# First attention: exponentials copied to the rounded type between queues, transposed one unit later, and one scratch space for all scores

## The chip, the cores and the metric

The kernel runs on one core of a Trainium2 chip. The metric is the device time of one execution in microseconds (us), the median of the runs shown. PE is the matrix engine (PEld its weight loads), ACT, DVE and POOL are the three engines for elementwise work, SP is the engine that issues most of the transfers (DMAs). Each engine has a list of instructions of its own, whose order is fixed when the program is built.

## The reference

One encoder layer for two sequences of 2048 tokens with 1024 features. What matters here:

```python
h = rms_norm(x, norm_w); proj = h @ w_in          # q_a k_a v_a g_a q_b k_b v_b g_b
o_a = windowed_gqa_sink(q_a, k_a, v_a, sink_a) * jax.nn.silu(g_a)   # "first attention"
o_b = neighbourhood_attn(q_b, k_b, v_b, rpb_b) * jax.nn.silu(g_b)   # "second attention"
x = x + jnp.concatenate([o_a, o_b], axis=-1) @ w_out
return x + (p @ w_ple) * jax.nn.sigmoid(x @ w_ple_gate)

# windowed_gqa_sink, for a block of 128 queries, 8 query heads, 2 key heads:
sc = jnp.einsum('bqkgd,bskd->bkgqs', qb, kb) * scale   # keys within +-128 tokens
sc = jnp.where(valid, sc, -jnp.inf)
m = jnp.maximum(jnp.max(sc, axis=-1, keepdims=True), sink_f)
e = jnp.exp(sc - m)
denom = jnp.sum(e, axis=-1, keepdims=True) + jnp.exp(sink_f - m)
o = jnp.einsum('bkgqs,bskd->bqkgd', e / denom, vb)
```

Everything is 32-bit. The kernel keeps that precision by splitting each operand of a product into a rounded high part (the type `float32r`, "the rounded type") and a low part, and adding the products of the parts.

## The kernel before

**Three stretches.** The first attention fills the first 750 us or so, the second attention runs to about 1800 us, and the output products fill the rest. This case is about the first.

**Tiles and units.** The first attention takes the 4096 tokens in 32 tiles of 128 (index `f`; `t` is the tile within its sequence of 16). Each tile has two units, one for each key head (`kv` 0 and 1). A tile whose neighbours on both sides exist (`left and right`) has the full window; four tiles of the 32 lie at an end of a sequence. In a unit (`unit_a`):

- `sc(i)`, i = 0 to 3: two products give the scores of 128 rows by 320 keys into PSUM; DVE (`softmax`, L295) adds the mask, writes the scores to SBUF and takes the row maximum. Two calls make a pair of 640 columns. After the fourth, `exps` runs: DVE makes `nm`, the negated maximum (L316), and ACT makes four exponentials in place (L319).
- `pt(j)`, j = 0 to 2: PE transposes the exponentials in blocks of 128x128 into PSUM (`tr`, L282): two blocks for j = 0, four for j = 1 and four for j = 2, ten in all. ACT copies them out as the high part of `pr` (L757) and DVE subtracts to make the low part (L759). For j = 0 both go in two halves of 64 partitions.
- `po(j)`: the products of `pr` with the values `vv`, high part then low part: four products of 256 columns for j = 0 and for j = 1, two of 512 columns for j = 2.
- `den`: the reciprocal of the denominator and the gate (`g2`). `fin`: PE transposes `g2` (`pgt`), ACT and DVE fold the halves of `po` and multiply, SP stores the result (`oa_d`).
- `prep` (once per tile): PE transposes the next tile's queries (`pqt`), `rest` finishes their split.

**The filler.** Between these steps PE works on the projections of a later tile, as a stream of products: `pk` (24 of 256 columns), `pq` and `pg` (24 of 512 columns each). Their operands come from `xr`, a split tile of x, loaded by SP (`stx`, and `stn` for the sums of squares).

**What sets the order.** A table `PLAN_A` gives for each step its place within the unit, as a share of the stream's cost, and whether it belongs to this unit (`now` = 1) or to the unit before it (0). So a step is put into PE's order behind so many products of the stream. The order of the other engines follows from a scheduler at build time that keeps data dependencies and the priorities of the program. What it made of ACT's and DVE's lists is shown below with the change.

**The types of a transpose.** `tr` transposes data of the type that it finds. In the first attention the exponentials are plain 32-bit floats; in most units of the second attention (`copied_`) ACT issues a DMA that copies each exponential into a tile `tn` of the rounded type (L328), and PE transposes that (L280).

**Buffers.** The scores of the first attention lie in `s2` (three slots of 640 columns). A tag `s` of five buffers of 512 columns serves early loads, the scores of the second attention and results of the last stretch. PSUM has three buffers for `sc`, `pt` and `pgt`, and two for `po`, `pqt` and the keys (`pkt`).

Of the kernel before, what the change touches and what calls it, by code (L numbers as in the profile page):

```python
# [58 lines left out]
def bias_offsets():  # L59
# [31 lines left out]
CP = 2  # L91
KB = 23
PLAN_A = (
    (0.04, 1, "sc", 0), (0.10, 1, "sc", 1), (0.12, 1, "sc", 2), (0.12, 1, "rest", 0), (0.14, 1, "sc", 3),
    (0.14, 1, "rest", 1), (0.14, 0, "po", 0),
    (0.22, 0, "po", 1), (0.34, 0, "po", 2), (0.45, 0, "fin", 0), (0.46, 1, "prep", 0), (0.58, 1, "den", 0),
    (0.75, 1, "pt", 0), (0.79, 1, "pt", 1), (0.88, 1, "pt", 2),
)
PLAN_B = (
# [13 lines left out]
    return 2 * NT <= f and not (4 * NT - 9 <= f < 4 * NT - 5 or f >= 6 * NT - 9)  # L113


def plan(f):

    def of(k):
        return PLAN_A if k < 2 * NT else PLAN_C if copied_(k) else PLAN_B
    if f <= 2 * NT:  # L120
        return of(f)
    return sorted([x for x in of(f - 1) if not x[1]] + [x for x in of(f) if x[1]], key=lambda x: x[0])


def emit(ctx, tc, io):
# [12 lines left out]
    rowwise = cp.tile([128, 128], F32R, tag="rowwise", name="rowwise")  # L138
    nc.gpsimd.tensor_copy(rowwise.rearrange("p (r c) -> p r c", c=16), ident.rearrange("p (c r) -> p r c", r=8))
# [8 lines left out]
    wkt = cp.tile([128, 4], F32, tag="wkt", name="wkt")  # L148
    nc.scalar.dma_start(wkt, io["qk_norms"])

    main = ctx.enter_context(tc.tile_pool(name="main", bufs=1))
# [139 lines left out]
    def softmax(i, ps, n, bias, sm, s=None):  # L291

        if s is None:
            s = main.tile([128, 512], F32, tag="s", name="s", bufs=SB)[:, :n]
        nc.vector.tensor_tensor_reduce(out=s, in0=ps[:, :n], in1=bias, scale=1.0, scalar=-3.0e38,  # L295
                                       op0=ALU.add, op1=ALU.max, accum_out=sm["mx"][:, i:i + 1])
        sm["s"].append(s)
# [70 lines left out]
        loads += [("n", f, 0), ("n", f, 1)] if f < 2 * NT else []  # L368
    loads, staged = iter(loads), {}

    def load_block(key, tag, bufs):
        kind, f, i = key
        staged[key] = main.tile([128, 512], F32, tag=tag, name="st" + kind, bufs=bufs)
# [61 lines left out]
    for i in range(2):  # L435
        raws_x += load_first(st[1][:, 2 * i:2 * i + 2], 4 + 2 * i, 0, 256)
    for i in range(2):
        load_block(("x", 1, i), "s", SB)
    raws_q += load_first(main.tile([128, 2, 512], F32, tag="p_t", name="ws", bufs=3), 0, 256, 512)
    raw = ap.tile([128, 4, 512], F32, tag="raw", name="ws", bufs=1)  # L440
    raws_q += load_first(raw[:, 0:2], 2, 256, 512)
    raws_q += load_first(raw[:, 2:4], 4, 256, 512)
    raws_q += load_first(main.tile([128, 2, 512], F32, tag="p_t", name="ws", bufs=3), 6, 256, 512)
    for i in range(2):
        load_block(("n", 0, i), "s", SB)
    for j in range(4):
        raws_g += load_first(ap.tile([128, 1, 512], F32, tag="qg", name="wg", bufs=6), j, 768, 512)
    cs = main.tile([128, 2, NT, 16], F32, tag="s", name="cs", bufs=SB)
    nc.sync.dma_start(cs, io["rope"])
    rw = ap.tile([128, 4, 16], F32, tag="rw", name="rw")  # L450
    nc.sync.dma_start(rw, io["rope_w"].partition_broadcast(128))
# [251 lines left out]
        qrest[f] = split_q(pqt, q1, q2, 1)  # L703
        return q1, q2

    p_rot, s2, tn = [], [], []

    def unit_a(f, kv):
        s, t = divmod(f, NT)
# [63 lines left out]
        def fin(_):  # L773
# [9 lines left out]
            for e in range(2):  # L783
# [2 lines left out]
            nc.vector.tensor_tensor(out=ot, in0=pgt, in1=ot, op=ALU.mult)  # L786
            nc.sync.dma_start(oa_d[s].rearrange("(i p) q -> p i q", p=128)[:, 2 * kv:2 * kv + 2, 128 * t:128 * t + 128],
                              ot)
        return {"sc": sc, "pt": pt, "po": po, "fin": fin, "prep": lambda _: nxt(f) if kv else None,
                "den": lambda _: next(got["ex"]), "rest": lambda _: None if kv else next(qrest[f])}  # L790

    pending = []
# [271 lines left out]
    def ple_ahead(n, tail=False):  # L1064

        load_p(n + 1)
        for m in range(KT):
            if m % 4 == 3 and (n < 3 or m == 3):
                load_coming()
            ps = ptile([128, TW], "pj", "pple")  # L1070
            if m == 5 and n + 1 < len(tiles):
                split_p(n + 1)
            flush("p0")
            for k in range(2):
                w, c = early["p"][2 * (m // 4) + k], 128 * (m % 4)
                for i, (a, b) in enumerate(((0, 0), (0, 1), (1, 0))):
                    mm(ps, w[:, a, c:c + 128], p_rs[n][:, k, b], k == 0 and i == 0, k == 1 and i == 2)
                    yield 215
            if tail:
                ev = main.tile([128, TW], F32, tag="s", name="ev", bufs=SB)  # L1080
            else:
                if not evs:
                    evs.extend([ap.tile([128, 3, 640], F32, tag="ev", name="ev", bufs=1), 0])
                if m // 2 % 2:
                    ev = ap.tile([128, TW], F32, tag="sq", name="ev", bufs=2)
                else:
                    ev = evs[0][:, evs[1] % 3, :TW]
                    evs[1] += 1
            P(nc.scalar.copy(ev, ps))
            store_ple(1)  # L1090
            if tail:
                nc.sync.dma_start(ple_d[n][:, m], ev)
            else:
                made.append((ple_d[n][:, m], ev))
# [72 lines left out]
    for f in range(6 * NT):  # L1167
# [7 lines left out]
        spent = 0  # L1175
        for kv in range(2 if in_a else 1):
            unit = unit_a(f, kv) if in_a else unit_b(f)
            for part, now, act, i in plan(f):
# [6 lines left out]
        while spent < total:  # L1185
            spent += next(stream, total)
        if f in (2 * NT - 1, 6 * NT - 1):
            for part, now, act, i in PLAN_A if in_a else PLAN_B:
# [14 lines left out]
    with tc.tile_pool(name="c", bufs=1, reuse_waits="tile") as op:  # L1203
# [132 lines left out]
        def result(n, i, mi, ps):  # L1336
# [3 lines left out]
            first, final = i not in (1, 4, 5), i not in (0, 2, 3)  # L1340
            V = nc.vector
            if first:
                r = main.tile([128, TW], F32, tag="s", name="r", bufs=SB) if count[1] % 9 < SB else \
# [164 lines left out]
```

## Time and profile before

| | us |
|---|---|
| median of three runs (2453.13 to 2453.51) | 2453.3 |
| profiled execution | 2451.72 |
| its span, first to last instruction | 2449.9 |
| busy: PE / PEld | 2437.0 / 2061.1 |
| busy: DVE / ACT / POOL | 1706.2 / 1413.3 / 851.0 |

The span is what the profile shows instruction by instruction; the profiled execution's own time is 1.8 us more, and the median of the runs 1.6 us more than that. PE counts as busy for 99% of the span, but its instructions overlap in the record: a transpose is recorded with 272 ns, and four in a row start about 109 ns apart. What an instruction costs PE is the distance from its start to the next start, not its recorded duration.

### The profile page before, as it was taken

What the parts mean: (1) busy time and instruction counts of PE and PEld (TensorE: products, weight loads), DVE (VectorE), ACT (ScalarE), POOL (GpSimd) and SP (SyncE); (2) the same over time, 40 slices, a digit from 0 to 9 for tenths busy, and PEclk for the clock granted to TensorE, in tenths of its full rate; (3) what the DMA queues carried; (4) which work ended last, traced back from release to release, by engine and by line L of the source; (5) the groups of instructions that cost most, each with busy time, mean ns of one, the idle gap of its engine ahead of it and who ended that gap; (6) DMA issues with size and microseconds to landing.
All of it is one profiled execution on the core that took longest, in us unless ns stands there. A gap on an engine that the chain in (4) does not pass through costs nothing.

```text
span 2449.9 us, 40820 instructions
## 1 busy us (share of the span) xinstructions
PE 2437.0 (99%) x13062; PEld 2061.1 (84%) x13062; DVE 1706.2 (70%) x4214; ACT 1413.3 (58%) x3408; POOL 851.0 (35%) x1363
## 2 busy tenths in 40 slices
PE   9999999999999999999999999999999999999999
PEld 8888888888888888888888888888888888888887
DVE  7777777777775666666666677776537655677776
ACT  7777767776755555666656666666753222344443
POOL 4555555555543544555444444443100000000000
PEclk9999999999999999999999999999999999999999
DMA  6323223232353677768966687787887445855765
GB/s 229 123 97 100 92 92 103 94 95 89 104 181 125 209 240 246 235 213 261 309 213 227 224 271 261 247 266 248 302 273 259 162 157 183 268 184 203 249 224 171
DMA packets 275254, 479.64 MB, mean 196 GB/s; under 512 B 31168, under 2 KB 116064, under 8 KB 270816
## 3 DMA queue, kind: packets, MB, share of 16 engines
q1 hardware_dynamic: 245376, 437.84, 53.8%
q10 hardware_dynamic: 29664, 39.19, 5.2%
q8 instruction: 104, 1.70, 0.3%
q14 instruction: 110, 0.90, 0.1%
HBM read 307.72 MB, written 134.23 MB: 180 GB/s over the span
## 4 chain that ended last, share of the span: by engine, by line
PE 91%; DVE 3%; DMA 3%; ACT 2%; POOL 1%; issue 1%; SPq 0%; DVEq 0%; ACTq 0%; POOLq 0%
PE pvg L276 15%; PE pqk L276 14%; PE acca L1311 14%; PE accc L1311 10%; PE pq L276 6%; PE pg L276 6%; PE scb L276 3%; PE pob L276 3%; PE po L276 3%; PE pple L276 3%; PE pk L276 3%; PE sc L276 3%; PE pt L282 2%; PE ptb L280 2%; DMA vw<-v_d 1%; DVE pr L759 1%
## 5 line engine op out<-in xcount | busy, mean ns | idle before, releaser
L276 PE MATMUL pvg<-wb,xr 128*128 128x512 f32 x1536 | 470.4, 408 | 0.3 <-DMA wb<-sp_1wb 0.3
L276 PE MATMUL pqk<-wa,xr 128*128 128x512 f32 x1536 | 431.1, 408 | 0.0
L319 ACT ACTIVATE s<-s,nm 128x320 f32<-128x320 f32 (+6 forms) x512 | 293.2, 574 | 148.5 <-DVE nm L316 118.0
L276 PEld LDWEIGHTS pvg<-wb,xr 128*128 128x128 f32 x1536 | 273.0, 189 | 33.2 <-DMA wb<-sp_1wb 0.8
L276 PEld LDWEIGHTS pqk<-wa,xr 128*128 128x128 f32 x1536 | 265.0, 188 | 39.2
L1293 ACT CAST opd<-raw 128x512 fp32r<-128x512 f32 x224 | 131.5, 619 | 270.7 <-PE acca L1311 117.8
L397 POOL TENSOR_TENSOR xr<-stx,xr 128x512 fp32r<-128x512 f32 x186 | 238.0, 1296 | 103.5 <-ACT xr L396 72.9
L1294 DVE TENSOR_TENSOR opd<-raw,opd 128x512 fp32r<-128x512 f32 x224 | 146.4, 685 | 146.2 <-ACT opd L1293 146.2
L276 PE MATMUL pg<-wb,xr 128*128 128x512 f32 x768 | 233.4, 410 | 1.3 <-DVE vv L554 1.0
L276 PE MATMUL pq<-wa,xr 128*128 128x512 f32 x768 | 219.3, 400 | 0.0
L295 DVE CUSTOM_DVE_ANT_0 s<-scb,bias 128x288 f32<-128x288 f32 (+3 forms) x256 | 138.8, 547 | 71.8 <-PE scb L276 51.6
L993 ACT COPY otb<-pob 64x512 f32<-64x512 f32 x128 | 74.3, 581 | 182.7 <-PE pob L276 182.0
L1311 PE MATMUL accc<-opd,wb 128*128 128x512 f32 x768 | 176.7, 389 | 0.0
L1311 PE MATMUL acca<-opd,wa 128*128 128x512 f32 (+1 forms) x780 | 175.9, 386 | 0.5 <-ACT r L1389 0.5
L1311 PE MATMUL acca<-opd,s 128*128 128x512 f32 x768 | 175.4, 389 | 0.0
L1311 PEld LDWEIGHTS acca<-opd,wa 128*128 128x128 f32 x780 | 145.0, 188 | 30.2 <-ACT r L1389 0.7
L1311 PEld LDWEIGHTS acca<-opd,s 128*128 128x128 f32 x768 | 144.1, 188 | 29.9
L1311 PEld LDWEIGHTS accc<-opd,wb 128*128 128x128 f32 x768 | 144.1, 188 | 29.9
L161 POOL TENSOR_TENSOR yb<-vrb,power 128x8 f32<-128x8 f32 x64 | 106.4, 1662 | 150.6 <-DVE vrb L831 137.7
L276 PEld LDWEIGHTS pq<-wa,xr 128*128 128x128 f32 x768 | 135.1, 189 | 17.3
L759 DVE TENSOR_TENSOR pr<-pt,pr 128x512 fp32r<-128x512 f32 (+2 forms) x248 | 135.3, 549 | 16.5 <-ACT pr L757 13.1
L276 PEld LDWEIGHTS pg<-wb,xr 128*128 128x128 f32 x768 | 131.9, 189 | 17.4 <-DVE vv L554 1.4
(177 smaller groups left out, 5141.4 us busy)
## 6 DMA issues: line engine op xcount, KB each, us to landing
stx<-x_b SPq DMA_DIRECT2D x128, 256.0 KB
vw<-v_d SPq DMA_DIRECT2D x96, 256.0 KB
stx<-x_a SPq DMA_DIRECT2D x64, 256.0 KB
stn<-x_n SPq DMA_DIRECT2D x64, 256.0 KB
v_d<-vb SPq DMA_DIRECT2D x64, 256.0 KB
ple_d<-ev SPq DMA_DIRECT2D x64, 256.0 KB
xres<-x_r SPq DMA_DIRECT2D x64, 256.0 KB
x_d<-r SPq DMA_DIRECT2D x64, 256.0 KB
```

The lines of the kernel that those rows point to most:

```text
L161: nc.gpsimd.tensor_tensor(out=y, in0=v, in1=power.broadcast_to([128, n]), op=ALU.pow)
L276: pinned(nc.tensor.matmul(out, lhsT, rhs, start=start, stop=stop))
L280: pinned(nc.tensor.transpose(out.bitcast(F32R), in_, eye))
L282: pinned(nc.tensor.transpose(out, in_, eye.bitcast(F32)))
L295: nc.vector.tensor_tensor_reduce(out=s, in0=ps[:, :n], in1=bias, scale=1.0, scalar=-3.0e38, op0=ALU.add, op1=ALU.max, accum_out=sm["mx"][: ...
L319: ex = nc.scalar.activation(ss[i], ss[i], AF.Exp, bias=nm[:, i:i + 1], accum_out=den[:, i:i + 1])
L397: low.tensor_tensor(out=lo, in0=raw, in1=hi.bitcast(F32), op=ALU.subtract)
L759: nc.vector.tensor_tensor(out=pr[r, 1, to], in0=pt[r, c], in1=pr[r, 0, to].bitcast(F32), op=ALU.subtract)
L993: nc.scalar.copy(ot[a:a + 64], pq[z:z + 64])
L1293: P(nc.scalar.copy(hi, v))
L1294: P(nc.vector.tensor_tensor(out=lo, in0=v, in1=hi.bitcast(F32), op=ALU.subtract))
L1311: pinned(nc.tensor.matmul(ps[:, cols], w[k][:, a, c:c + 128], o[:, b, cols], start=i in (0, 1, 4) and k == 0 and j == 0, stop=k == 3 and j ...
```

## The change

In tiles with both neighbours, the exponentials of a pair (128x640) are copied by a DMA that SP issues (`turn`) into a tile `tna` of the rounded type, three slots of 640 columns, and the transposes read that. The copies are ordered at 0.39 of the unit; `pt` moves from 0.75 to 0.88 of the same unit to 0.24, 0.31 and 0.38 of the next one; `po` moves from 0.14, 0.22 and 0.34 of the next unit to 0.52, 0.60 and 0.72; `fin` from 0.45 to 0.80, `prep` from 0.46 to 0.66 and `den` from 0.58 to 0.74. The places of `sc` become 0.04, 0.08, 0.11, 0.14. The four end tiles make no copy and are transposed as before in type, at the new places. The last unit keeps `pt` within itself (`PLAN_L`).

`tna` takes the room of `s2`. The scores of the first attention now lie in four slots of 640 columns of one tile `space`, which also replaces the five buffers of the tag `s` everywhere (`s_tile`). The identity matrix is built in that space and kept in the rounded type.

```diff
 PLAN_A = (
-    (0.04, 1, "sc", 0), (0.10, 1, "sc", 1), (0.12, 1, "sc", 2), (0.12, 1, "rest", 0), (0.14, 1, "sc", 3),
-    (0.14, 1, "rest", 1), (0.14, 0, "po", 0),
-    (0.22, 0, "po", 1), (0.34, 0, "po", 2), (0.45, 0, "fin", 0), (0.46, 1, "prep", 0), (0.58, 1, "den", 0),
+    (0.04, 1, "sc", 0), (0.08, 1, "sc", 1), (0.11, 1, "sc", 2), (0.12, 1, "rest", 0), (0.14, 1, "sc", 3),
+    (0.14, 1, "rest", 1), (0.24, 0, "pt", 0), (0.31, 0, "pt", 1), (0.38, 0, "pt", 2), (0.39, 1, "turn", 0), (0.39, 1, "turn", 1),
+    (0.52, 0, "po", 0), (0.60, 0, "po", 1), (0.66, 1, "prep", 0), (0.72, 0, "po", 2), (0.74, 1, "den", 0), (0.80, 0, "fin", 0),
+)
+PLAN_L = tuple((part, now or act == "pt", act, i) for part, now, act, i in PLAN_A if act != "pt") + (
     (0.75, 1, "pt", 0), (0.79, 1, "pt", 1), (0.88, 1, "pt", 2),
 )
...
-    ident = cp.tile([128, 128], F32, tag="ident", name="ident")
-    make_identity(nc, ident)
...
+    space = main.tile([128, SB * 512], F32, tag="s", name="s")
+    taken = [0]
+
+    def s_tile():
+
+        k = taken[0] % SB
+        taken[0] += 1
+        return space[:, 512 * k:512 * k + 512]
+
+    eye32 = space[:, 512 * SB - 128:512 * SB]
+    make_identity(nc, eye32)
+    ident, rowwise = (cp.tile([128, 128], F32R, tag=n, name=n) for n in ("ident", "rowwise"))
+    nc.vector.tensor_copy(ident, eye32)
...
+        def turn(pair):
+
+            if left and right:
+                if len(s2) < 3:
+                    s2.append(ap.tile([128, 3, 640], F32R, tag="ev", name="tna", bufs=1))
+                to = s2[2][:, s2[1] % 3]
+                s2[1] += 1
+                nc.sync.dma_start(to.bitcast(F32), pairs[pair])
+                pairs[pair] = to
+
         def sc(i):
...
             if half == 0:
-                if not s2:
-                    s2.extend([ap.tile([128, 3, 640], F32, tag="ev", name="s2", bufs=1), 0])
-                pairs.append(s2[0][:, s2[1] % 3])
-                s2[1] += 1
+                k = 640 * (s2[0] % 4)
+                pairs.append(space[:, k:k + 640])
+                s2[0] += 1
```

How the rows of three engines move. PE, in the unit of key head 0 of an inner tile, from the last scores to the first value products (`pq` is the filler); before:

```order
L276 MATMUL sc<-ks_a,q_292 128x320
L276 MATMUL po<-pr,vv 128x256 x4
L276 MATMUL pq<-wa_106,xr 128x512
L276 MATMUL pq<-wa_107,xr 128x512
L276 MATMUL po<-pr,vv 128x256 x4
L276 MATMUL pq<-wa_107,xr 128x512 x2
L276 MATMUL pq<-wa_108,xr 128x512 x2
L276 MATMUL po<-pr,vv 128x512 x2
```

and with the change:

```order
L288 MATMUL sc<-ks_a,q_289 128x320
L288 MATMUL pq<-wa_108,xr 128x512
L288 MATMUL pq<-wa_109,xr 128x512 x2
L292 MATMUL pt<-ident,tna 128x128 x2
L288 MATMUL pq<-wa_109,xr 128x512
L288 MATMUL pq<-wa_110,xr 128x512
L292 MATMUL pt<-ident,tna 128x128 x4
L288 MATMUL pq<-wa_110,xr 128x512 x2
L292 MATMUL pt<-ident,tna 128x128 x4
L288 MATMUL pq<-wa_111,xr 128x512 x3
L288 MATMUL pq<-wa_112,xr 128x512
L288 MATMUL po<-pr,vv 128x256 x4
```

The value products used to follow the last scores at once, with transposes made in the unit before; now the transposes of the unit before stand between them, with eleven filler products from the last scores to the first `po`, and three from `po(0)` to `po(1)`. In the unit of key head 1 the list is alike with `pg` as filler: also eleven up to `po(0)`, then two of `pg` and one of `pk` up to `po(1)`.

ACT, the same unit (`s` are the exponentials, `pr` the copies out of the transposes); before:

```order
L354 CAST q_2991<-pqt 64x512
L319 ACTIVATE s_656,den<-s_656,nm 128x320 x4
L334 ACTIVATE es<-es 128x4
L782 COPY ot<-po 64x2x2x64 x2
L553 ACTIVATE vv<-pk,y 128x2x64
L757 CAST pr<-pt 64x256 x2
L599 ACTIVATE sq<-pq 128x512
L757 CAST pr<-pt 128x512 x2
```

and with the change, first in the unit of key head 0 and then in that of key head 1:

```order
L366 CAST q_4880<-pqt 64x512
L331 ACTIVATE s,den<-s,nm 128x320 x4
L346 ACTIVATE es<-es 128x4
L778 CAST pr<-pt 64x256 x2
L778 CAST pr<-pt 128x512 x2
L565 ACTIVATE vv<-pk,y 128x2x64
L803 COPY ot<-po 64x2x2x64 x2
```

```order
L534 ACTIVATE ks_a<-pkt,wk 64x128 x2
L778 CAST pr<-pt 64x256 x2
L331 ACTIVATE s,den<-s,nm 128x320 x4
L346 ACTIVATE es<-es 128x4
L778 CAST pr<-pt 128x512 x2
```

Behind the exponentials of a unit ACT used to copy `po` out; now it copies the transposes of the unit before: in the unit of key head 0 all four copies stand behind the four exponentials, in that of key head 1 the two copies of `pt(1)` and `pt(2)` do.

DVE, the unit of key head 0 with the change, from `nm` on (`gs` is a gate, 128x512):

```order
L328 SCALAR_TENSOR_TENSOR nm<-mx,snk 128x4
L345 TENSOR_TENSOR es<-snk,nm 128x4
L368 TENSOR_TENSOR q_289<-pqt,q_3015 64x512
L581 TENSOR_SCALAR vr<-ssq,ee 128x2
L780 TENSOR_TENSOR pr<-pt,pr 64x256 x2
L649 SCALAR_TENSOR_TENSOR gs<-gs,pg 128x512
L780 TENSOR_TENSOR pr<-pt,pr 128x512 x2
```

The subtractions of `pt(0)` come first, then the gate, then those of `pt(1)` and `pt(2)`. Before, the gate stood behind the first of the unit's four softmax steps, and these subtractions stood at the end of the unit before. In the unit of key head 1, with the change, DVE's list from `nm` on reads `q<-pq` (128x512), `es`, the two halves of `pt(0)`, `pt(1)` and `pt(2)`; ahead of `nm` stand two subtractions for the keys (`ks_a`), as before.

More of the change, by code (lines that the diff above doesn't have):

```diff
@@ L113, in copied_, with plan, of @@
     return 2 * NT <= f and not (4 * NT - 9 <= f < 4 * NT - 5 or f >= 6 * NT - 9)
[L116 to L122, printed above, removed]
+def plan(f, kv):
+    def of(k, kv):
+        if k < 2 * NT:
+            return PLAN_L if (k, kv) == (2 * NT - 1, 1) else PLAN_A
+        return PLAN_C if copied_(k) else PLAN_B
+    back = (f, 0) if kv else (max(f - 1, 0), 1)
+    return sorted([x for x in of(*back) if not x[1]] + [x for x in of(f, kv) if x[1]], key=lambda x: x[0])
 def emit(ctx, tc, io):
@@ L133, in ptile @@
         return pp.tile(shape, F32, tag=tag, name=name, bufs=PSB[tag])
-    ident = cp.tile([128, 128], F32, tag="ident", name="ident")
-    make_identity(nc, ident)
-    rowwise = cp.tile([128, 128], F32R, tag="rowwise", name="rowwise")
-    nc.gpsimd.tensor_copy(rowwise.rearrange("p (r c) -> p r c", c=16), ident.rearrange("p (c r) -> p r c", r=8))
+    main = ctx.enter_context(tc.tile_pool(name="main", bufs=1))
+    space = main.tile([128, SB * 512], F32, tag="s", name="s")
[8 more added lines that the diff above has]
+    nc.vector.tensor_copy(ident, eye32)
+    nc.gpsimd.tensor_copy(rowwise.rearrange("p (r c) -> p r c", c=16), eye32.rearrange("p (c r) -> p r c", r=8))
     nw = cp.tile([128, KT], F32, tag="nw", name="nw")
@@ L293, in softmax @@
         if s is None:
-            s = main.tile([128, 512], F32, tag="s", name="s", bufs=SB)[:, :n]
+            s = s_tile()[:, :n]
         nc.vector.tensor_tensor_reduce(out=s, in0=ps[:, :n], in1=bias, scale=1.0, scalar=-3.0e38,
@@ L369, in emit, with load_block @@
     loads, staged = iter(loads), {}
-    def load_block(key, tag, bufs):
+    def load_block(key, tag=None, bufs=None):
         kind, f, i = key
-        staged[key] = main.tile([128, 512], F32, tag=tag, name="st" + kind, bufs=bufs)
+        staged[key] = main.tile([128, 512], F32, tag=tag, name="st" + kind, bufs=bufs) if tag else s_tile()
         if kind == "n":
@@ L444, in emit @@
     for i in range(2):
[L445 removed]
+        load_block(("n", 0, i))
     for j in range(4):
         raws_g += load_first(ap.tile([128, 1, 512], F32, tag="qg", name="wg", bufs=6), j, 768, 512)
[L448 removed]
+    cs = s_tile().rearrange("p (a t c) -> p a t c", a=2, c=16)
     nc.sync.dma_start(cs, io["rope"])
@@ L1079, in ple_ahead @@
             if tail:
-                ev = main.tile([128, TW], F32, tag="s", name="ev", bufs=SB)
+                ev = s_tile()
             else:
@@ L1177, in emit @@
             unit = unit_a(f, kv) if in_a else unit_b(f)
-            for part, now, act, i in plan(f):
+            for part, now, act, i in plan(f, kv):
                 at = (kv + part) / (2 if in_a else 1)
@@ L1187, in emit @@
         if f in (2 * NT - 1, 6 * NT - 1):
-            for part, now, act, i in PLAN_A if in_a else PLAN_B:
+            for part, now, act, i in PLAN_L if in_a else PLAN_B:
                 if not now:
@@ L1342, in result @@
             if first:
-                r = main.tile([128, TW], F32, tag="s", name="r", bufs=SB) if count[1] % 9 < SB else \
+                r = s_tile() if count[1] % 9 < SB else \
                     op.tile([128, TW], F32, tag="r", name="r", bufs=9 - SB)
```

7 lines of the change are left out of this document (3 added, 4 removed).

## Prediction

> **What bounds the kernel now.** I read the busy times first, then the stretch of the first attention alone, then what PE waited for there.
>
> ```profile
> PE 2437.0 (99%) x13062; PEld 2061.1 (84%) x13062; DVE 1706.2 (70%) x4214; ACT 1413.3 (58%) x3408; POOL 851.0 (35%) x1363
> 60.00:300.00 240.00, 240.00 (x1455) 211.16 (x1454) 187.38 (x582) 170.83 (x481) 127.28 (x269) 1.00 0.32 103
> PE pg L276 <- DVE vv L554: 1.0, 1, 1.0
> PEld sc L276 <- DVE pr L759: 5.9, 28, 0.4
> ```
>
> The second row is a stretch of inner tiles in the columns PE, PEld, DVE, ACT, POOL: PE is covered for all of its 240 us, DVE for 78%, ACT for 71%, at the full granted clock. The other two rows are the longest waits of PE and of its loads between 60 and 745 us: microseconds in all, times, longest. So the first attention runs at the pace of PE's list: a nanosecond taken off PE's work there is gained, and a nanosecond for which the next product waits on ACT or DVE is lost, whatever the shares of these two engines.
>
> **What the rounded type saves.** The timeline of PE has starts (first column) that price an instruction by the distance to the next start. First the present transposes among `pg` products, with rows that price the filler and the products around them; then rounded ones in the second attention.
>
> ```profile
> 314.62 0.94 PE L276 MATMUL pg<-wb,xr 128*128 128x512 f32 x3
> 315.40 0.60 PE L282 MATMUL pt<-ident,s 128*128 128x128 f32 x4
> 315.75 1.40 PE L276 MATMUL pg<-wb,xr 128*128 128x512 f32 x5
> 317.00 0.46 PE L276 MATMUL sc<-ks_a,q 128*128 128x320 f32 x2
> ...
> 318.85 0.45 PE L276 MATMUL sc<-ks_a,q 128*128 128x320 f32 x2
> 319.14 0.64 PE L276 MATMUL po<-pr,vv 128*128 128x256 f32 x4
> 319.61 0.63 PE L276 MATMUL pg<-wb,xr 128*128 128x512 f32 x2
> ...
> 320.55 1.08 PE L276 MATMUL pg<-wb,xr 128*128 128x512 f32 x4
> 321.46 0.61 PE L276 MATMUL po<-pr,vv 128*128 128x512 f32 x2
> ```
>
> ```profile
> 886.98 0.46 PE L280 MATMUL ptb<-rowwise,tn 128*128 128x128 f32 x4
> ...
> 889.57 0.46 PE L280 MATMUL ptb<-rowwise,tn 128*128 128x128 f32 x4
> ...
> 1176.02 2.27 PE L276 MATMUL pqk<-wa,xr 128*128 128x512 f32 x9
> 1178.12 0.33 PE L276 MATMUL scb<-ks_b,q1b 128*128 128x360 f32 x1
> ```
>
> A filler product costs 0.23 us (321.46 less 320.55, over 4; 2.10 over 9 in the second attention, 0.233). Three of them and four plain transposes take 1.13, so a plain transpose costs (1.13 - 0.69)/4 = 0.11. From 886.98 to 889.57 lie two rounds of four rounded transposes and four fillers: (2.59/2 - 0.93)/4 = 0.091. The 28 inner tiles have 2 units of 10 transposes, 560 in all: 560 x 0.018 = 10 us saved. The bounds are nothing and, by the recorded durations,
>
> ```profile
> L282 PE MATMUL pt<-ident,s 128*128 128x128 f32 (+1 forms) x624 | 99.5, 272 | 0.8 <-DVE ot L786 0.4 <-DVE den L336 0.3
> L280 PE MATMUL ptb<-rowwise,tn 128*128 128x128 f32 (+2 forms) x660 | 78.0, 231 | 0.0
> ```
>
> 560 x 41 ns = 23 us. I take 10, since starts are what PE's list is paced by. The new places also part the scores from the transposes that held their PSUM buffers; at most the 5.9 us above goes, and I take 4.
>
> The Trainium skill (TensorE: Matmul & The Clock Gate, Part 2, on LDWEIGHTS) gives a weight load a time by its columns alone, 107 ns for 128, whatever the type. The plain 0.11 agrees with that, the rounded 0.091 does not; by the rule the type would save nothing, which is the third rival below.
>
> **What the moves cost.** All else rests on when the copies of a transpose are ready and when `po` comes. Before, `pt` was made some four microseconds ahead of `po`, with the unit's own exponentials long done. Now the transposes of the unit before fall into the time in which ACT makes this unit's exponentials, and ACT's list has these first. Rows of ACT and of DVE around two units, the first of key head 0 and the second of key head 1:
>
> ```profile
> 309.48 0.56 ACT L319 ACTIVATE s<-s,nm 128x320 f32<-128x320 f32 x1 [2.34 <-DVE nm L316]
> ...
> 311.77 0.73 ACT L782 COPY ot<-po 64x256 f32<-64x256 f32 x2
> ...
> 314.24 0.76 ACT L757 CAST pr<-pt 64x256 fp32r<-64x256 f32 x2
> ...
> 315.51 1.17 ACT L757 CAST pr<-pt 128x512 fp32r<-128x512 f32 x2
> ...
> 320.81 0.56 ACT L319 ACTIVATE s<-s,nm 128x320 f32<-128x320 f32 x1 [1.26 <-DVE nm L316]
> ```
>
> ```profile
> 307.32 0.68 DVE L637 SCALAR_TENSOR_TENSOR gs<-gs,pg 128x512 f32<-128x512 f32 x1
> ...
> 308.74 0.49 DVE L295 CUSTOM_DVE_ANT_0 s<-sc,mask 128x320 f32<-128x320 f32 x1
> ...
> 315.02 0.85 DVE L759 TENSOR_TENSOR pr<-pt,pr 64x256 fp32r<-64x256 f32 x2 [0.32 <-ACT pr L757]
> ...
> 316.63 0.69 DVE L759 TENSOR_TENSOR pr<-pt,pr 128x512 fp32r<-128x512 f32 x1
> ...
> 319.34 0.49 DVE L295 CUSTOM_DVE_ANT_0 s<-sc,mask 128x320 f32<-128x320 f32 x1
> ```
>
> The four exponentials hold ACT for 2.29 (309.48 to 311.77). From the last softmax to the first exponential it takes 0.74 (308.74 to 309.48), and from the start of the last scores on PE to that softmax 0.49 (318.85 to 319.34).
>
> *Key head 0*, time from PE's start of the last scores. PE: scores 0.29, eleven fillers 2.53, ten transposes 0.91, so the first `po` product comes at 3.73. ACT: exponentials from 0.49 + 0.74 = 1.23 to 3.52, then the halves of `pt(0)` to 3.90 and 4.28, `pt(1)` to 4.87. DVE: the halves of `pt(0)` from 3.93 to 4.35 and 4.78. The four products take 0.12 each, in the order high, low, high, low; the second waits for 4.39, the fourth for 4.82, and they end at 4.94 instead of 3.73 + 0.47 = 4.20. Lost: 0.74. Three fillers later, at 5.63, comes `po(1)`: DVE made the gate from 4.78 to 5.46 and `pt(1)`'s low part to 6.15, so its second product waits until 6.19 and the step ends at 6.55, not 6.10. Lost: 0.45. Late next is nothing: `pt(2)` is done at 6.84, ahead of `po(2)` at 7.24.
>
> *Key head 1.* Here ACT has `pt(0)` before the exponentials. PE makes these transposes behind the scores and three fillers, at 0.98 to 1.16, and ACT can begin at about 1.4 (a transpose's 0.27 and the hand-over) and ends at 2.14; the scores allow the exponentials from 1.96 on (318.85 to 320.81), so they run from 2.14 to 4.43, and `pt(1)` is copied to 5.02, its low part made to 5.75. `po(0)` comes at 3.73 and is served (DVE did both halves by 3.7). `po(1)` comes two fillers of 0.23 and a `pk` product of half that width later, at 4.78; it waits for the high part until 5.06 and for the low one until 5.79, and ends at 6.15 instead of 5.25. Lost: 0.90.
>
> Together 2.1 us a tile. A product that really waited has its weight load bared too, which I put at 0.1 for the pair; 2.2. Behind the waiting `po` on PE stand the fillers and the next scores, so the delay passes to everything in the tile. Each kind of unit is met 31 times: 68 us. My times may be off by 0.3 in either unit, which is 19 us over all.
>
> **What costs nothing.** The 112 copies move 320 KB each with DMA engines that are 0.32 busy in this stretch. The second attention shows such copies (180 KB) and their use:
>
> ```profile
> 914.14 0.47 ACTq L328 DMA_DIRECT2D tn<-s  x1
> 918.65 0.36 PE L280 MATMUL ptb<-rowwise,tn 128*120 128x128 f32 x3
> ```
>
> 4.5 us sufficed there with no wait. Here the exponentials end 3.5 or 4.4 us behind the last scores and the transposes come some 13 us behind them, so about 9 us are there; a copy later than that would cost its lateness in each unit. Behind a waiting copy on SP stand the loads `stx` and `stn` and the stores; by the table the next of them is placed 0.4 of a unit behind the copies, some 3 us after the exponentials end. At the handover to the second attention the copies share SP's queue with the weights of these rows (transfers and the size of each), 8 MB in all, with the same 9 us of room:
>
> ```profile
> wa<-sp_0wa SPq DMA_DIRECT2D x8, 512.0 KB
> wb<-sp_0wb SPq DMA_DIRECT2D x8, 512.0 KB
> ```
> ACT, DVE and POOL do the same instructions as before but for the identity's one copy at the start, and from the second attention on the lists of PE and ACT hold the same work in the same order; I allow 2 us either way.
>
> **The sum.** -10 - 4 + 68 = +54 on the span of 2449.9: 2504, or 2506 as that execution's own time. The median of the runs is 1.6 above that execution, so 2453.3 + 54 = **2507 us**.
>
> **The rivals.**
>
> - *The waits don't arise: faster.* The place is the same `po(0)` and `po(1)`; it decides if `pr` is ready some 1.1 us earlier than I find, or PE comes as much later. For it: PE never waited there before, and 78% of DVE leaves room. Against: the exponentials' 2.29 us stand ahead of the copies in ACT's list, which no share of idle time alters. 2453.3 - 14 = 2439. Chance 0.13.
> - *Half of the waits.* Each of the eleven fillers at 0.25 instead of 0.23 (1.25 over 5 from 315.75 to 317.00 would be that) brings `po` 0.2 later, and an earlier softmax as much again: 1.2 lost a tile, 37 - 14 = +23, 2476. Chance 0.17.
> - *The type saves nothing.* Both types' weight loads are recorded alike (140 and 136 ns, the rows below), and if these set the pace among fillers the 10 us stay: 2517. Chance 0.06. The Trainium skill's rule on LDWEIGHTS above would have it so.
> - *The copies are late.* If SP issues them behind a load that waits, and they land 10 us behind the exponentials, each unit waits about 1 us more: +60, 2567. Chance 0.03.
> - *It evens out* within 0.2% (5 us, about what the runs of this kernel can tell from no change). Chance 0.03.
>
> ```profile
> L282 PEld LDWEIGHTS pt<-ident,s 128*128 128x128 f32 (+1 forms) x624 | 76.3, 140 | 13.7 <-issue 1.7 <-DVE ot L786 0.6
> L280 PEld LDWEIGHTS ptb<-rowwise,tn 128*128 128x128 f32 (+2 forms) x660 | 75.7, 136 | 28.7
> ```
>
> My forecast has 0.58. Its own range is 2488 to 2526; with the half case and the third rival 2462 to 2532, which leaves out 0.19. Faster 0.13, same 0.03, slower 0.84.
>
> **What would show it.** Two rows of one kind, a tile apart, give a tile's time of 22.4 us now:
>
> ```profile
> 300.62 0.60 PE L282 MATMUL pqt<-ident,q 128*128 128x128 f32 x4
> ...
> 323.05 0.60 PE L282 MATMUL pqt<-ident,q 128*128 128x128 f32 x4
> ```
>
> Right: PE's waits in the first attention are headed by `po` waiting for DVE `pr` and ACT `pr`, 50 us or more in all, with a repeating gap at `po(0)` and `po(1)` of key head 0 and at `po(1)` of key head 1; a tile takes 24.3 us or so instead of 22.4; `pt` starts 0.09 apart; no wait on `tna`. Wrong: tiles of 22.1 us and no `po` among the waits; or `pt` waiting on the DMA; or a difference that lies behind 760 us.

## The result and the profile after

The changed kernel takes 2519.7 us (median; 2518.2 to 2524.2) where the kernel before takes 2453.2: 1.0275 times as long, 95% interval 1.0257 to 1.0293. That is 66 us more, where 54 more were forecast. The profiled execution of the changed kernel has a span of 2522.4 us and a time of its own of 2524.2.

Busy time over the span from the page of the changed kernel, then the stretch of inner tiles that was shown of the kernel before (columns PE, PEld, DVE, ACT, POOL, granted clock, DMA share, GB/s):

```profile
PE 2470.0 (98%) x13062; PEld 2054.6 (81%) x13062; DVE 1718.2 (68%) x4215; ACT 1426.3 (57%) x3408; POOL 851.0 (34%) x1363
```

```profile
60.00:300.00 240.00, 228.08 (x1321) 188.50 (x1320) 171.95 (x525) 159.95 (x440) 115.17 (x244) 1.00 0.44 147
```

PE, which was covered for all of the 240 us, now has 12 us bare, and starts 1321 instructions where it started 1455. DVE and ACT are less busy in this stretch as well. Over the whole span the numbers of instructions are the same but for one of DVE, and the two are recorded only 12 and 13 us busier: little was added, something got later. What PE waited for between 60 and 830 us, and what its weight loads waited for (us in all, times, longest):

```profile
PE po L288 <- DVE pr L780: 22.4, 56, 0.5
PE po L288 <- ACT pr L778: 8.4, 31, 1.3
PE pt L292 <- DMA tna<-s: 2.0, 1, 2.0
```

```profile
PEld po L288 <- DVE pr L780: 51.5, 117, 0.9
PEld po L288 <- ACT pr L778: 33.7, 58, 1.7
```

The two rows of `po` are new; in the kernel before no such row was among the longest. The loads tell more than the products here: their two rows make 85 us, those of the products 31, and the lost time below comes to 79. A tile's time by two rows of one kind on PE:

```profile
301.68 0.60 PE L294 MATMUL pqt<-ident,q 128*128 128x128 f32 x4
...
326.52 0.60 PE L294 MATMUL pqt<-ident,q 128*128 128x128 f32 x4
```

That is 24.84 us, 2.4 more than the 22.4 before. The median distance over the inner tiles, from first `pk` to first `pk`, is 24.83 against 22.48: 2.35 us in each of 28 tiles, 66 us. In the profiled executions, of which that of the change is the slowest of its four runs, the last `po` of the first attention starts at 823.5 instead of 753.0; from there to the end both spans take nearly the same, 1698.9 and 1696.9 us. So the time went into the first attention, tile by tile.

Where in the tile: PE from the last scores of key head 0, then of key head 1.

```profile
307.11 0.46 PE L288 MATMUL sc<-ks_a,q 128*128 128x320 f32 x2
...
308.22 0.70 PE L288 MATMUL pq<-wa,xr 128*128 128x512 f32 x2
308.76 0.45 PE L292 MATMUL pt<-ident,tna 128*128 128x128 f32 x4
309.05 0.70 PE L288 MATMUL pq<-wa,xr 128*128 128x512 f32 x2
...
309.88 1.15 PE L288 MATMUL pq<-wa,xr 128*128 128x512 f32 x4
311.17 0.39 PE L288 MATMUL po<-pr,vv 128*128 128x256 f32 x1
312.02 0.85 PE L288 MATMUL po<-pr,vv 128*128 128x256 f32 x3 [0.46 <-DVE pr L780]
312.70 0.86 PE L288 MATMUL pq<-wa,xr 128*128 128x512 f32 x3
313.40 1.02 PE L288 MATMUL po<-pr,vv 128*128 128x256 f32 x4
314.26 0.86 PE L288 MATMUL pq<-wa,xr 128*128 128x512 f32 x3
...
319.64 0.45 PE L288 MATMUL sc<-ks_a,q 128*128 128x320 f32 x2
...
323.42 0.63 PE L288 MATMUL po<-pr,vv 128*128 128x256 f32 x4
323.89 0.63 PE L288 MATMUL pg<-wb,xr 128*128 128x512 f32 x2
324.36 0.28 PE L288 MATMUL pk<-wx,xr 128*128 128x256 f32 x1
324.85 0.39 PE L288 MATMUL po<-pr,vv 128*128 128x256 f32 x1 [0.22 <-ACT pr L778]
325.57 0.62 PE L288 MATMUL po<-pr,vv 128*128 128x256 f32 x3 [0.34 <-DVE pr L780]
326.04 0.64 PE L288 MATMUL pk<-wx,xr 128*128 128x256 f32 x4
```

Read the starts. Four `po` products without a wait take 0.47 (323.42 to 323.89). Key head 0: the four fillers ahead of `po(0)` start at 309.88. In key head 1, where nothing waits, the same four take 1.00 (322.42 to 323.42). So `po(0)` arrives at 310.88 and is over at 312.70, 1.82 later instead of 0.47: 1.35 lost. `po(1)` takes 0.86 (313.40 to 314.26): 0.39 lost. Key head 1: `po(0)` waits for nothing; `po(1)` arrives at 324.48 and is over at 326.04, 1.56: 1.09 lost. Together 2.83 us a tile, 79 us over 28 tiles.

And the two engines that make `pr`, ACT and then DVE, in the same two units:

```profile
308.34 0.56 ACT L331 ACTIVATE s<-s,nm 128x320 f32<-128x320 f32 x1 [2.20 <-DVE nm L328]
...
310.54 0.19 ACT L346 ACTIVATE es<-es 128x4 f32<-128x4 f32 x1
310.75 1.86 ACT L778 CAST pr<-pt 64x256 fp32r<-64x256 f32 x4
...
321.79 0.56 ACT L331 ACTIVATE s<-s,nm 128x320 f32<-128x320 f32 x1
...
324.21 1.07 ACT L778 CAST pr<-pt 128x512 fp32r<-128x512 f32 x2
```

```profile
311.55 0.88 DVE L780 TENSOR_TENSOR pr<-pt,pr 64x256 fp32r<-64x256 f32 x2 [2.07 <-ACT pr L778]
...
324.83 1.29 DVE L780 TENSOR_TENSOR pr<-pt,pr 128x512 fp32r<-128x512 f32 x2 [1.68 <-ACT pr L778]
```

In key head 0 the copies out of `pt` follow directly on the exponentials (310.54 and 310.75), though PE had begun the transposes before 308.22. In key head 1 those out of `pt(1)` do (324.21).

### The profile page after: what moved, and what is told of

The parts are those of the page before. It is cut to its first block, busy times and chain, and to the rows that moved or that the text cites. A ratio compares the mean times of both kernels' runs of the same rounds, so it can differ in the third digit from the quotient of the medians.

```text
span 2522.4 us, 41352 instructions
## 1 busy us (share of the span) xinstructions
PE 2470.0 (98%) x13062; PEld 2054.6 (81%) x13062; DVE 1718.2 (68%) x4215; ACT 1426.3 (57%) x3408; POOL 851.0 (34%) x1363
## 4 chain that ended last, share of the span: by engine, by line
PE 82%; DVE 6%; ACT 6%; DMA 2%; issue 2%; POOL 0%; ACTq 0%; SPq 0%; DVEq 0%
PE pvg L288 14%; PE pqk L288 13%; PE acca L1332 13%; PE accc L1332 10%; PE pg L288 5%; ACT s L331 4%; PE pk L288 4%; PE scb L288 3%; PE pob L288 3%; PE pple L288 3%; PE pq L288 3%; PE po L288 3%; PE sc L288 2%; DVE pr L780 2%; PE ptb L292 2%
## 5 line engine op out<-in xcount | busy, mean ns | idle before, releaser
L288 PE MATMUL pq<-wa,xr 128*128 128x512 f32 x768 | 235.8, 402 | 0.0
L288 PE MATMUL po<-pr,vv 128*128 128x256 f32 (+1 forms) x608 | 153.8, 336 | 37.6 <-DVE pr L780 22.4
L288 PEld LDWEIGHTS po<-pr,vv 128*128 128x128 f32 x608 | 98.5, 189 | 93.6 <-DVE pr L780 51.5
```

The costliest lines, as they stand in the source:

```text
L288: pinned(nc.tensor.matmul(out, lhsT, rhs, start=start, stop=stop))
```

## The experiments

Three theories stood against each other at first. Mine: `po` waits because ACT's list has the four exponentials ahead of the copies out of the transposes. A: the copies' traffic is the cause (the DMA engines' share in the stretch went from 0.32 to 0.44). B: the one space makes work wait for work that it has nothing to do with. A fourth, C, came up on the way: scores, transposes and gates share three PSUM buffers, and these take back what is won at `po`. "Tile" is the median distance of the inner tiles' first `pk` products; ratios are to the kernel before, run beside each, whose median was 2453.2 for the change and 2452.5 to 2452.8 for the experiments.

| kernel | tile, us | median (range), us | ratio, 95% interval |
|---|---|---|---|
| before | 22.48 | 2453.2 | 1 |
| the change | 24.83 | 2519.7 (2518.2 to 2524.2) | 1.0275 (1.0257 to 1.0293) |
| space_only | 22.48 | 2452.2 (2451.4 to 2458.0) | 1.0004 (0.9995 to 1.0014) |
| no_copies | 24.90 | 2522.2 (2521.4 to 2525.6) | 1.0280 (1.0263 to 1.0297) |
| later_products | 22.76 | 2468.3 (2465.0 to 2471.5) | 1.0061 (1.0046 to 1.0076) |
| own_unit | 23.37 | 2488.4 (2486.0 to 2490.1) | 1.0142 (1.0127 to 1.0157) |
| only_po_later | 22.82 | 2459.9 (2459.1 to 2464.9) | 1.0029 (1.0017 to 1.0040) |
| only_po_later_plain | 23.00 | 2466.7 (2464.1 to 2469.6) | 1.0050 (1.0033 to 1.0067) |
| only_pt_earlier | 22.53 | 2457.5 (2455.1 to 2460.0) | 1.0018 (1.0009 to 1.0027) |
| pt_earlier_po1_later | 22.54 | 2456.8 (2451.9 to 2459.7) | 1.0014 (1.0004 to 1.0023) |
| spread | 21.93 | 2438.9 (2437.2 to 2442.3) | 0.9943 (0.9929 to 0.9957) |
| spread_plain | 22.32 | 2446.7 (2445.4 to 2448.4) | 0.9973 (0.9964 to 0.9983) |

### space_only: one part of the change alone

Against the kernel before; the rest of the space as in the change's diff, without `turn` and with the old table:

```diff
-                pairs.append(s2[0][:, s2[1] % 3])
-                s2[1] += 1
+                k = 640 * (s2[0] % 4)
+                pairs.append(space[:, k:k + 640])
+                s2[0] += 1
```

> The kernel before, with one part of the change: the scores of the first attention lie in the one space that the other score tiles share (four places of 640 columns), and the identity is rounded; no copies, the transposes in the plain type and at their old places. Theory (the products wait because ACT makes four exponentials ahead of the copies out of the transposes): nothing of that order is touched, so 2453 us, within 5. Rival A (the copies' traffic slows the work): 2453 too. Rival B (the one space makes work wait for work that it does not need): 2500 us or more, with waits of DVE or PE on the scores' tile s in the first attention.

Measured: 2452.2 us, no difference, and the same tile. Theory B falls: the one space costs nothing.

### no_copies: the change without its copies

```diff
         def turn(pair):

-            if left and right:
+            if False:
```

> The changed kernel without its copies: the transposes stay where the change puts them, but read the scores where they lie, in the plain type. Theory: the order on ACT is that of the changed kernel, so the po products wait as they do there. The ten transposes take 0.18 us more a unit, but in a unit that waits the wait is that much shorter; so 2520 us, at most 10 more. Rival A (the copies' traffic is the cause): the cause is gone, 2463 us or less (the plain type costs up to 10 us). Rival B (the one space): 2520 us, but then space_only is slow too.

Measured: 2522.2 us, 2.5 above the change. The cause is still there with the copies gone, so theory A falls. PE from the last scores of key head 0:

```profile
307.59 0.46 PE L288 MATMUL sc<-ks_a,q 128*128 128x320 f32 x2
...
310.54 1.17 PE L288 MATMUL pq<-wa,xr 128*128 128x512 f32 x4
311.67 0.38 PE L288 MATMUL po<-pr,vv 128*128 128x256 f32 x1
312.51 0.84 PE L288 MATMUL po<-pr,vv 128*128 128x256 f32 x3 [0.46 <-DVE pr L780]
313.19 0.86 PE L288 MATMUL pq<-wa,xr 128*128 128x512 f32 x3
```

`po(0)` arrives at 310.54 + 1.00 = 311.54, 3.95 behind the last scores, where the change has it at 3.77: the ten plain transposes are 0.18 slower, as priced. But it ends at 5.60 behind them, where the change ends at 5.59. The wait is shorter by just what the transposes are longer. So at its own places the change does not even gain the type: 20 transposes a tile at 0.018 would be 0.36, and the tiles differ by 0.07.

### later_products and own_unit: the waits of `po` taken away in two ways

later_products moves the products back, own_unit brings the transposes to the end of their own unit and leaves the products where the kernel before has them. In later_products the last unit of the first attention makes its transposes ahead of the last products of the unit before it, which then multiply the wrong probabilities; the work done is the same.

```diff
 later_products
-    (0.52, 0, "po", 0), (0.60, 0, "po", 1), (0.66, 1, "prep", 0), (0.72, 0, "po", 2), (0.74, 1, "den", 0), (0.80, 0, "fin", 0),
+    (0.66, 1, "prep", 0), (0.70, 0, "po", 0), (0.74, 1, "den", 0), (0.86, 0, "po", 1), (0.90, 0, "po", 2), (0.95, 0, "fin", 0),
```

```diff
 own_unit
-    (0.14, 1, "rest", 1), (0.24, 0, "pt", 0), (0.31, 0, "pt", 1), (0.38, 0, "pt", 2), (0.39, 1, "turn", 0), (0.39, 1, "turn", 1),
-    (0.52, 0, "po", 0), (0.60, 0, "po", 1), (0.66, 1, "prep", 0), (0.72, 0, "po", 2), (0.74, 1, "den", 0), (0.80, 0, "fin", 0),
+    (0.14, 1, "rest", 1), (0.145, 0, "po", 0),
+    (0.22, 0, "po", 1), (0.34, 0, "po", 2), (0.39, 1, "turn", 0), (0.39, 1, "turn", 1), (0.45, 0, "fin", 0), (0.46, 1, "prep", 0), (0.58, 1, "den", 0),
+    (0.88, 1, "pt", 0), (0.92, 1, "pt", 1), (0.97, 1, "pt", 2),
```

(In own_unit the scores also stand at 0.10 and 0.12 for 0.08 and 0.11, as in the kernel before.)

> The changed kernel with its three po steps moved back by 0.16 to 0.26 of a unit (0.70, 0.86 and 0.90 for 0.52, 0.60 and 0.72) and fin to 0.95, copies and rounded type kept. In the written order ACT then has the four exponentials behind the first copies of the transposes in most units, and po comes 2 us or more behind the last of the three pr. Theory: po waits no more, a tile takes 22.1 to 22.5 us for 24.8, and the whole 2439 to 2453 us. Rival A (traffic) and rival B (space): nothing that they name is changed, so 2510 to 2525 us, and the lost time shows at other instructions of PE.

> Copies and rounded type kept, but the transposes at the end of their own unit (0.88, 0.92 and 0.97, some 8 us behind the last scores), and po, fin, prep and den where the kernel before has them. ACT then makes the copies of the transposes ahead of the next unit's exponentials, as in the kernel before. Theory: no po waits on pr; the rounded type's 0.018 us on each of 560 transposes is then seen, so 2439 to 2447 us. The copies end 6 to 7 us behind the last scores (they land 2.8 us behind their issue in the median), so few waits of pt on tna, 5 us in all. Rival A (traffic): 2500 us or more, as with the change. Rival B (space): 2510 us or more.

Measured: 2468.3 and 2488.4 us. Both win back much of the loss, which rivals A and B did not allow, and both miss what I expected, by 15 and 41 us. What PE waited for between 60 and 790 us, later_products first, own_unit second:

```profile
PE sc L288 <- DVE ot L807: 8.8, 33, 1.1
```

```profile
PE sc L289 <- DVE pr L781: 10.4, 29, 1.1
PE pt L293 <- DMA tna<-s: 9.3, 9, 4.7
```

The waits of `po` are gone but for 2 us in later_products, as I said. But the scores wait instead: for `ot` where the gate's transposes (`fin`) come right ahead of the next scores, for `pr` where the transposes do. Scores, transposes and gates take turns in three PSUM buffers, and each buffer is free only when DVE has read it; with the steps close together DVE is behind. I had left that out of both expectations. These rows do not explain all of it: in own_unit the weight loads of the scores waited longest for a tile of POOL, `rd` (15.6 us, where `pr` has 12.9), and why was not followed up. In own_unit the transposes wait for the copies too: 8 us were not always enough.

### only_po_later: nothing but the products moved, and by less

```diff
-    (0.52, 0, "po", 0), (0.60, 0, "po", 1), (0.66, 1, "prep", 0), (0.72, 0, "po", 2), (0.74, 1, "den", 0), (0.80, 0, "fin", 0),
+    (0.66, 0, "po", 0), (0.74, 0, "po", 1), (0.66, 1, "prep", 0), (0.80, 0, "po", 2), (0.74, 1, "den", 0), (0.84, 0, "fin", 0),
```

> The changed kernel with nothing but its po steps and fin later: 0.66, 0.74 and 0.80 for 0.52, 0.60 and 0.72, fin at 0.84 for 0.80. The written order of the transposes' copies and the exponentials on ACT, and of the subtractions on DVE, is that of the change. Theory: po(0) comes 1.5 us later in the unit, at 5.3 us behind the last scores of key head 0 where the last part that it needs was seen ready at 5.3, po(1) at 6.7 where 6.6 is needed (key head 1: 5.8); so no waits to speak of, a tile of 22.1 to 22.3 us, 2439 to 2446 us. Rival C (it is the three PSUM buffers that scores, transposes and gates share, which showed as waits of sc in later_products and own_unit; the waits then only move from po to sc): a tile of 22.7 us or more, 2460 to 2500 us, with waits of sc on pr, mx or ot of 25 us or more.

> The kernel of only_po_later without its copies, the transposes reading the scores in the plain type. With no waits to absorb a difference this prices the rounded type: by the starts (0.110 against 0.092 us a transpose, 560 of them) 10 us more than only_po_later. Rival (the type saves nothing, a transpose's weight load taking the same whatever its type): the same time within 2 us. Rival A (the copies cost time by their traffic): less than only_po_later.

Measured: 2459.9 us, 60 less than the change and 14 above the upper end that I expected. Two waits are left, both in key head 0:

```profile
309.57 0.46 PE L288 MATMUL sc<-ks_a,q 128*128 128x320 f32 x2
...
314.30 1.02 PE L288 MATMUL po<-pr,vv 128*128 128x256 f32 x4
315.15 0.86 PE L288 MATMUL pq<-wa,xr 128*128 128x512 f32 x3
315.85 1.02 PE L288 MATMUL po<-pr,vv 128*128 128x256 f32 x4
316.71 0.40 PE L288 MATMUL pq<-wa,xr 128*128 128x512 f32 x1
```

`po(0)` arrives 4.73 behind the last scores, not 5.3: the place in the table moved by 0.14 of a unit, but only 0.96 us lie between. It loses 0.38 where the change, arriving at 3.77, loses 1.35: 0.96 later, 0.97 less lost. That is the theory's own measure, one for one. The tile of 22.82 lies where rival C put it, but its sign is missing: the loads of the scores waited 2 us in all, not 25 or more, so rival C does not hold here.

The plain type costs 6.8 us more over the whole (2466.7). It too is partly eaten by the two waits, so this pair bounds the type's price from below only.

### only_pt_earlier and pt_earlier_po1_later: the order on ACT

```diff
 only_pt_earlier
-    (0.14, 1, "rest", 1), (0.24, 0, "pt", 0), (0.31, 0, "pt", 1), (0.38, 0, "pt", 2), (0.39, 1, "turn", 0), (0.39, 1, "turn", 1),
+    (0.14, 1, "rest", 1), (0.18, 0, "pt", 0), (0.24, 0, "pt", 1), (0.31, 0, "pt", 2), (0.39, 1, "turn", 0), (0.39, 1, "turn", 1),
```

```diff
 pt_earlier_po1_later, besides
-    (0.52, 0, "po", 0), (0.60, 0, "po", 1), (0.66, 1, "prep", 0), (0.72, 0, "po", 2), (0.74, 1, "den", 0), (0.80, 0, "fin", 0),
+    (0.52, 0, "po", 0), (0.66, 0, "po", 1), (0.66, 1, "prep", 0), (0.76, 0, "po", 2), (0.74, 1, "den", 0), (0.82, 0, "fin", 0),
```

> The changed kernel with nothing but its transposes earlier: 0.18, 0.24 and 0.31 for 0.24, 0.31 and 0.38; the po steps stay where the change has them. In the written order ACT now makes the copies out of pt(0) ahead of the four exponentials in both units, and those out of pt(1) in key head 1 too; pt(1) of key head 0 stays behind them. Theory (ACT's order is what makes po wait): the waits at po(0) of key head 0 and at po(1) of key head 1 go, the one at po(1) of key head 0 stays with some 0.5 us; a tile of 22.6 to 22.9 us, 2450 to 2465 us. If it were the place alone and not the order, 0.67 us of 2.4 would be won in each unit that waits: a tile of 23.5 to 24 us, 2480 to 2500 us. Rival C (shared PSUM buffers): waits of pt on the softmaxes' mx, 2490 us or more.

> As only_pt_earlier, with po(1) at 0.66 for 0.60, po(2) at 0.76 for 0.72 and fin at 0.82 for 0.80. Theory: po(1) of key head 0 now comes behind its probabilities too, so no wait of po is left: a tile of 22.1 to 22.4 us, 2439 to 2448 us. Rival C: as in only_pt_earlier, 2470 us or more.

Measured: 2457.5 us, within what I expected, and a tile of 22.53, just under it. The products stand where the change has them, the transposes 0.06 or 0.07 of a unit earlier, and 62 us of the 66 are back; the place alone could have given 40 at most by the expectation's bound. ACT and PE of only_pt_earlier in key head 0 (last scores at 305.98):

```profile
306.89 0.76 ACT L778 CAST pr<-pt 64x256 fp32r<-64x256 f32 x2 [1.88 <-PE pt L292]
307.67 0.56 ACT L331 ACTIVATE s<-s,nm 128x320 f32<-128x320 f32 x1
...
310.08 1.08 ACT L778 CAST pr<-pt 128x512 fp32r<-128x512 f32 x2
```

```profile
309.75 0.65 PE L288 MATMUL po<-pr,vv 128*128 128x256 f32 x4
310.24 0.86 PE L288 MATMUL pq<-wa,xr 128*128 128x512 f32 x3
310.94 0.28 PE L288 MATMUL po<-pr,vv 128*128 128x256 f32 x1
311.45 0.62 PE L288 MATMUL po<-pr,vv 128*128 128x256 f32 x3 [0.24 <-DVE pr L780]
```

The copies out of `pt(0)` are now ahead of the exponentials and `po(0)` runs through in 0.49; `pt(1)` is still behind them (310.08), and so `po(1)` still waits, 0.5 us, as expected. The exponentials themselves start 0.46 later than in the change (1.69 for 1.23 behind the last scores), and that costs nothing that these rows show.

With `po(1)` later as well the tile should have fallen to 22.1 to 22.4; it stayed at 22.54. `po(1)` came 0.14 us short of its low part, and with `fin` at 0.82 the scores' loads waited for `ot`, 9.2 us in 27 times: rival C is right about this part.

### spread: a version that beats both

```diff
-    (0.14, 1, "rest", 1), (0.24, 0, "pt", 0), (0.31, 0, "pt", 1), (0.38, 0, "pt", 2), (0.39, 1, "turn", 0), (0.39, 1, "turn", 1),
-    (0.52, 0, "po", 0), (0.60, 0, "po", 1), (0.66, 1, "prep", 0), (0.72, 0, "po", 2), (0.74, 1, "den", 0), (0.80, 0, "fin", 0),
+    (0.14, 1, "rest", 1), (0.16, 0, "pt", 0), (0.22, 0, "pt", 1), (0.28, 0, "pt", 2), (0.39, 1, "turn", 0), (0.39, 1, "turn", 1),
+    (0.50, 0, "po", 0), (0.68, 0, "po", 1), (0.62, 1, "prep", 0), (0.73, 0, "po", 2), (0.72, 1, "den", 0), (0.76, 0, "fin", 0),
```

spread_plain has besides it the edit of no_copies.

> The changed kernel with only numbers of its table moved: transposes at 0.16, 0.22 and 0.28 (as in only_pt_earlier, the copies out of pt(0) then stand ahead of the exponentials on ACT), po(1) at 0.68, where pt_earlier_po1_later still showed its low part 0.14 us late, and fin at 0.76, since there the scores of key head 1 waited for DVE's ot. Theory: with no wait left in the tile the rounded transposes are gained: 22.0 to 22.3 us for 22.5 before, 2438 to 2449 us, faster than the kernel before. Rival C (the shared PSUM buffers give a wait back wherever the steps stand): 22.5 us a tile, 2452 to 2458 us.

> The kernel of spread without its copies, the transposes reading the scores in the plain type; the written order on PE, ACT and DVE is the same. Theory: 0.018 us more on each of 560 transposes, 0.36 us a tile, 10 us over all against spread. If the type saves nothing: the same within 2 us. If the copies' traffic costs: less than spread.

Measured: 2438.9 us, 14 us faster than the kernel before and 81 faster than the change. A tile and its two first `po` steps in key head 0:

```profile
250.31 0.60 PE L294 MATMUL pqt<-ident,q 128*128 128x128 f32 x4
...
260.33 0.63 PE L288 MATMUL po<-pr,vv 128*128 128x256 f32 x4
260.79 1.30 PE L288 MATMUL pq<-wa,xr 128*128 128x512 f32 x5
261.93 0.64 PE L288 MATMUL po<-pr,vv 128*128 128x256 f32 x4
262.40 0.63 PE L288 MATMUL pq<-wa,xr 128*128 128x512 f32 x2
...
272.24 0.60 PE L294 MATMUL pqt<-ident,q 128*128 128x128 f32 x4
```

```profile
60.00:300.00 240.00, 240.00 (x1498) 212.48 (x1497) 197.24 (x592) 180.09 (x494) 128.20 (x275) 1.00 0.49 166
```

Both steps take 0.47 or less, the tile 21.93, and PE is covered for all of the 240 us again, with 1498 instructions where the kernel before starts 1455. With nothing left to absorb it, the plain type costs 7.8 us (2446.7) and 0.39 us a tile, 0.0195 for each of the 20 transposes. Over 28 tiles that is 10.9; some 3 us of it do not reach the end. In the profiled executions spread is 9.7 us ahead at the last `pk` and 7.1 at the last scores, so they are given back between these two, before the second attention. There `pt` waited 1.6 us in spread (for `nm` 1.1, for `tna` 0.5) and 0.3 in spread_plain, and the granted clock was 0.89 from 700 to 715 us in spread, where spread_plain has 1.00 throughout: an estimated 1.65 us (15 x 0.11). Together that is about the 2.6 of the profiled executions; whether the other runs lose it in the same way isn't shown. The DMA engines move 166 GB/s in this stretch against 103 in spread_plain, and the kernel that moves more is the faster one. The two differ in the type as well as in the copies, so a cost of the copies could hide in the type's gain; but the gain, 0.39 us a tile, is no less than the 0.36 that the starts had priced.

## Why the prediction was right, and where it was off

*What bounds.* Right. PE's list sets the pace: the waits of `po` went into the tile almost to their full size, as the next sum shows, and a tile without waits gains in full.

*The type and the old waits, -10 and -4.* Right in the kernel where they can be seen: spread's tile is 0.55 below the kernel before, 15.4 us over 28 tiles; 0.39 of it is the type (10.9 us), 0.16 is put down to the old waits (4.5, the tile of spread_plain against that of the kernel before; 5.9 was the most that could go). In the change itself they are there too, under the waits: 2.83 - 0.55 = 2.28, and the tile grew by 2.35.

*The waits at `po`, 2.2 us a tile and 31 tiles, 68 us.* The mechanism and the places were right: `po(0)` and `po(1)` of key head 0, `po(1)` of key head 1, none at `po(0)` of key head 1. The size was low: 2.83. By place, forecast and measured: 0.74 and 1.35; 0.45 and 0.39; 0.90 and 1.09; the forecast had 0.1 more for the bared weight loads of all. **The term that was mis-sized is the first, "DVE: the halves of `pt(0)` from 3.93".** Measured from the last scores DVE starts there at 4.44. I let DVE begin on the first half when ACT had copied that half; it begins when ACT has copied both (310.75 + 0.76 = 311.51, start 311.55). The row quoted in the prediction showed that already: 315.02 behind the copies of 314.24 to 315.00. That is 0.38. The other 0.12 is ACT: from the first exponential to the first copy 2.41, not 2.29. Up to `es`, the small instruction behind the four, both kernels take 2.20; but before, the next instruction started 0.10 behind `es` (311.67 to 311.77), and in the change the copy out of `pt` starts 0.21 behind it (310.54 to 310.75). I had carried over the 0.10; why the copy starts later isn't shown. The same 0.12 is most of what key head 1 was off. The arrivals were right to 0.06: 3.77 for 3.73 and 4.84 for 4.78.

*31 tiles.* Too many: the inner tiles, 28 of them, make up the 66. Counted with the measured sizes the sum is 28 x (2.83 - 0.55) = 64, where 66 were measured. The forecast of 54 had a wait too small by more than a fifth and a count too large by a tenth. These two errors work against each other, and that is luck: with 28 tiles and its own 2.2 the forecast would have been +48, further off.

*What costs nothing.* Right for the copies (no_copies, spread) and for the space (space_only), and for what lies behind the first attention, within 2 us. Not quite for the DMA: "no wait on `tna`" holds for every inner tile, but one copy at the handover came 2.0 us late.

*The rivals.* "The waits don't arise", 2439 us, is what spread does at 2438.9, by the condition that was named: `pr` ready earlier or PE there later. "Half of the waits" falls: `po` came at 3.77, not 0.2 later than forecast, and 2.83 us were lost a tile, not 1.2. "The copies are late" shows in one copy alone, and it did not even out. "The type saves nothing" falls: 7.8 us between spread_plain and spread, with the same order of work. The rule of the Trainium skill (TensorE: Matmul & The Clock Gate, Part 2, on LDWEIGHTS) goes by columns alone, and by it both types would take 107 ns; the traces here agree for the plain type (0.11) and not for the rounded one (0.092, from 308.22 to 309.05 less two fillers over four in the change).

*What would show it.* `po` waiting for `pr` heads PE's waits, at the three places. I asked for 50 us or more in all: the rows of PE's products have only 31, those of its weight loads 85, so the sign named the wrong rows. The tile is 24.8 for 24.3.

## What to carry to other kernels

When a step moves next to another on PE, look at the list of the engine that serves both: here a move of 0.06 or 0.07 of a unit decided if ACT made four exponentials (2.4 us) ahead of most of the copies that PE waited for, and won back 62 us. A gain on a bound engine is seen only where that engine does not wait behind it; price the saving and the wait apart, and measure the saving in a version without waits. And a wait taken away returns at the next shared thing, here the three PSUM buffers, unless the steps that use it are spread out.

## What was not expected of the hardware

A rounded transpose among the filler products costs 0.0195 us less than a plain one, although the loads of both are recorded alike in the kernel before (136 and 140 ns): the recorded duration did not tell the pace, the distance of the starts did. And DMA engines that are 0.49 busy instead of 0.32 in the same stretch, with copies from SBUF to SBUF among the loads, cost PE, ACT and DVE nothing that these runs can see.
